# Block 2: expert weights go into the out-projection's buffers one by one, and the overflow loop moves from pair 25 to pair 28

## The chip, the cores and the metric

The kernel runs on one core of one Trainium2 chip. The metric is the time of one execution in device microseconds (us). The kernel before takes 3347.88 us (median of three runs, 3345.87 to 3349.38).

## What is computed

Two transformer blocks on 1024 tokens of width 1024, in float32. The change touches only the end of the second block: the product with `w_mla_o`, the merge of two branches, the product with `w_out`, the router, and 64 experts of hidden width 256, of which every token takes two. Cut to this part, the reference is:

```python
branch_b = o @ w_mla_o                                   # inside mla_attention
merged = sigmoid(g_a) * branch_a + sigmoid(g_b) * branch_b
h = h + merged @ w_out
u = rmsnorm(h, norm2_g)
g_logits, e_logits = u @ wg + bg, u @ we + be            # 8 groups, 8 experts in each
# best group; its best two experts; their weights
...
y = (silu(xb @ w1[e]) * (xb @ w3[e])) @ w2[e]            # for each expert e, the rows of its tokens
h = h + sum over a token's two experts of weight * y
```

An expert gets as many rows as the router gives it. The kernel provides 64 slots for each expert, and a loop for the rows beyond them.

## The kernel before

**Merge phase** (`phase3`, lines 1398 to 1427). The tokens are taken in two halves `b` of 512, and for each the 1024 output columns in eight steps `m` of 128. A step needs a slab of `w_mla_o`, 1024 x 128. Float32 products are made from operands that are split in a high and a low part (`wh`, `wl`), so a step has 8 x 3 matmuls. `slab2` brings a slab: the weights come by DMA, issued on SP, into a staging tile `ws` of 128 x 512 (256 KB), in two parts; ACT casts a part to `wh`, DVE subtracts to get `wl`, and then the staging tile is free for the next load. A tag with `bufs=2` in a pool is a ring of two buffers, and a load into a ring waits until the buffer's last user is done. The staging tile has `sbufs=2`. The results of the merge stand in four tiles: `mT0h`, `mT0l` (half 0) and `mT1h`, `mT1l` (half 1), each 16 KB in a partition.

Within the same loops the four slabs `ws[0]` to `ws[3]` of `w_out` (1024 x 256 each, in four parts of 256 KB) are brought, one at the steps 8b+m = 2, 5, 8 and 11. Before, they are made in pool `p3x` with a staging ring of their own there, while the slabs of `w_mla_o` stage in pool `p3y`. So 32 loads of 256 KB go through the one ring and 16 through the other.

**Out-projection** (`out2`, lines 1846 to 1885). Eight tiles `t` of 128 tokens: 96 matmuls with `mT` and the four `w_out` slabs, norm, router logits, and after tiles 3, 6 and 7 a part of the routing (`route_group`). Tiles 0 to 3 read `mT0`, tiles 4 to 7 `mT1`. SP brings a row tile `o_x` for every `t`.

**Experts** (`moe2`, lines 1888 to 1985). 32 pairs `p` of experts; a pair's weights are six DMAs of 1 MB (6.29 MB): gate and up for two experts (`n_w`) and down for two (`n_d`). There are six `wt` and six `dt` buffers, so three pairs are held; the weights of pair `p + 3` are loaded from POOL's queue when pair `p` has been used. `wt[0]` lies apart, all others are in a pool that takes the room of `p3x`, so it opens when `out2` is over: the waits are by tile, and a buffer waits for the old tiles that lay in the same place. SP issues the loads of pairs 0 to 2, POOL the rest. The rows of a pair are gathered by POOL (`n_x`, line 1009), turned on PE (`tp`), multiplied (`mm`), passed through ACT and DVE (`n_h`), turned and multiplied again, scaled (`n_y`) and added to the result by an indirect DMA from POOL (line 1015, "scatter" below).

**Overflow loop** (`overflow`, lines 1019 to 1127): a hardware loop over the count `v_ni` of blocks of rows beyond the slots; each engine loads `v_ni` (line 1059) and branches (line 1060). With these inputs its body is never run. It stands behind pair 25's scatter, ahead of the loads of pair 28.

The scheduler that puts instructions in order on each engine is not the program text's; the orders shown below are those of the built program.

Of the kernel before, what the change touches and what calls it, by code (L numbers as in the profile page):

```python
# [67 lines left out]
class Kern:  # L68
# [106 lines left out]
    def phase1a(self, keep, dram):  # L175
        """Modulation, norm, the projections of the mixer, and its gated linear attention among them."""
# [8 lines left out]
        # gate of the mixer, shift and scale of the second norm, gate of the experts  # L185
        self.rows = self.t(dram, [4, D], tag="rows")

        with tc.tile_pool(name="p1a", bufs=1) as pool, tc.tile_pool(name="p1a_ps", bufs=1, space=PSUM) as psum:
# [436 lines left out]
    def da_units(self, pool, psum, cp):  # L625
        tc, nc, a = self.tc, self.nc, self.a
        # lambda
# [14 lines left out]
        for qb in range(4):  # L642
            for h in range(4):
# [282 lines left out]
        # the logits from rows that are not normed yet: scale and shift in the router's weights and bias  # L926
# [23 lines left out]
    def turned(self, pool, psum, x, bufs=2):  # L950
        """x [P, D] -> [P, 8, 128], every 128 columns transposed"""
# [9 lines left out]
    def logits(self, pool, psum, x, rs, rw, rb, out, n, tbufs=2):  # L961
        """out = rs * (x @ rw) + rb for a tile of tokens"""
# [23 lines left out]
    def turn_cols(self, pool, psum, x, n, tag, split, rows=P):  # L986
        """x [rows, 128 n] -> xT [P, n, rows], xT[p, k] the column p * n + k of x: in two parts or as it is"""
# [25 lines left out]
    def scatter(self, dst, idx, src):  # L1013
        """rows of src added to those of dst, every index once or out of bounds"""
# [4 lines left out]
    def overflow(self, pool, psum, pre, rt, h2d, yd, wg, wu, wd, E, HID, cap, gain=None):  # L1019
        """The slots of an expert past its first cap, 128 at a time."""  # L1020
# [136 lines left out]
    def moe1(self, rt):  # L1157
        """Every expert's slots against its weights, float32 products in two parts."""
# [102 lines left out]
    # ---------------------------------------------------------------- block 2, mixer  # L1261
    def slab2(self, pool, segs, kk, n, bufs=2, tag="w", sbufs=2, parts=2):
        """Weights [P, kk, n] from column segments of DRAM views [P, kk, w], split in two parts."""
        nc = self.nc
        wh = self.t(pool, [P, 8, 256], F32R, tag=tag + "h", bufs=bufs) if kk * n == 2048 else None
        if wh is None:
# [8 lines left out]
        for h in range(0, kk, step):  # L1275
            st = self.t(pool, [P, step * n], tag=tag + f"s{step * n}", bufs=sbufs).rearrange("p (k n) -> p k n", k=step)
# [10 lines left out]
    def proj_T(self, psum, w, col, x, kk, fin):  # L1287
        """fin(token block, [P, 512] of W[:, col:col+128].T @ x), x [P, kk, S] and w split"""
# [8 lines left out]
    def phase3(self, dram, rt2_pool, close_m1, out):  # L1297
# [20 lines left out]
        with tc.tile_pool(name="p3u_ps", bufs=1, space=PSUM, reuse_waits="tile") as psum:  # L1318
# [4 lines left out]
            # recurrent branch  # L1323
# [3 lines left out]
            # gates of the two branches, and the recurrent branch's way out  # L1327
# [57 lines left out]
        # attention  # L1385
# [10 lines left out]
        # way out  # L1396
        with tc.tile_pool(name="p3x", bufs=1, reuse_waits="tile") as pool:
            mT = [[self.t(pool, [P, 8, 512], F32R, tag=f"mT{b}{n}") for n in "hl"] for b in range(2)]
            with tc.tile_pool(name="p3y", bufs=1, side="right", reuse_waits="tile") as p2, \
# [4 lines left out]
                for b in range(2):  # L1404
# [7 lines left out]
                    for m in range(8):  # L1412
# [16 lines left out]
            self.m2_w = [self.t(self.m2r_cm.__enter__(), [P, 2, 8, 256], tag="n_w0")]  # L1429
# [3 lines left out]
    def norms(self, pool, psum, uT, wi, z):  # L1433
        """The norms between the blocks, u in two parts, and its low-rank products z."""
# [14 lines left out]
        for t in range(NT):  # L1449
# [9 lines left out]
            # the second norm, of x rs: its sum of squares from that of x  # L1459
# [18 lines left out]
    def low_rank(self, pool, mq, psum, z, zT, kss, gz, t):  # L1478
        """The normed low-rank rows of a tile of tokens, turned and in two parts."""
# [18 lines left out]
    def lru(self, pool, wp, psum, uT, wi, gd):  # L1498
        nc, a = self.nc, self.a
        # c1 = -4 softplus(-lambda), softplus as max(x, 0) + log1p(exp(-|x|))  # L1500
# [27 lines left out]
        for f in range(8):  # L1528
# [19 lines left out]
            # a, and -expm1(2 log a) as tanh(-log a) (1 + a^2)  # L1548
# [10 lines left out]
            # gelu  # L1559
# [21 lines left out]
    def rope_tables(self, pool, mq):  # L1581
        """cos and sin of position * frequency, [P, NT, 32] each"""
# [304 lines left out]
    def moe2(self, rt):  # L1887
# [4 lines left out]
        with tc.tile_pool(name="m2w", bufs=1, reuse_waits="tile") as wp:  # L1892
# [40 lines left out]
            for p in range(2):  # L1933
                load(p)
# [110 lines left out]
```

## Time and profile before

| what | value |
|---|---|
| median of 3 runs | 3347.88 us (3345.87 to 3349.38) |
| span of the profiled execution | 3342.7 us; no time of its own is given beside the span, 5.2 us less than the median |
| PE busy | 2993.7 us, 90% of the span |
| DVE, ACT, POOL busy | 1768.0, 1370.7, 835.8 us |
| DMA | 705.55 MB, 211 GB/s over the span |
| the last quarter: merge 2540 to 2641, out-projection to 2763, routing to 2784, experts to 3342.7 | 802.7 us |

Times of the trace are microseconds from the span's start. An engine's busy time in a stretch says how full it is there; what it waits for is read from the rows that name the end of an idle time. PEclk is the granted TensorE clock as a share of 2.4 GHz. Where the DMA share is near 1, the 16 DMA engines have no room.

### The profile page before, as it was taken

The page shows a single profiled execution, that of the slowest core. Times are in us where ns is not written, and L with a number is a line of the kernel's source. Part 1 is how long each engine was busy: PE and PEld are TensorE (multiplying, and loading weights), DVE is VectorE, ACT ScalarE, POOL GpSimd, SP SyncE. Part 2 cuts the span into 40 slices and gives each one's busy share as a digit, 9 for nine tenths or more (in the row PEclk, how much of TensorE's full clock was granted, in tenths as well). Part 3 has the DMA queues.
Part 4 walks back from the last instruction along what each step waited for, and adds up shares of the span by engine and source line. Part 5 has one row for each costly group of instructions (what it writes and reads, how often), then busy time and mean ns, then how long its engine had stood idle before and what let it go on. Part 6 is the DMA issues. An engine that isn't in the chain of part 4 may idle for free.

```text
span 3342.7 us, 42770 instructions
## 1 busy us (share of the span) xinstructions
PE 2993.7 (90%) x15849; PEld 2195.4 (66%) x15849; DVE 1768.0 (53%) x3374; ACT 1370.7 (41%) x2247; POOL 835.8 (25%) x553
## 2 busy tenths in 40 slices
PE   7999999799978899889799999999998997877858
PEld 4988854677756666666487778788887893332323
DVE  4244332877668778778656731348886443111101
ACT  4345311555535566566556632236664211000001
POOL 1000011122223468767510000110001103333332
PEclk8999999799989899999899999999999998999979
DMA  6223376666569899899732253332235549999988
GB/s 212 91 80 95 92 226 198 178 166 173 137 225 317 285 330 343 285 359 343 234 118 76 76 208 96 120 96 73 69 83 179 178 173 346 407 386 363 390 334 301
DMA packets 282097, 705.55 MB, mean 211 GB/s; under 512 B 33760, under 2 KB 168060, under 8 KB 233116
## 3 DMA queue, kind: packets, MB, share of 16 engines
q1 hardware_dynamic: 231036, 462.13, 42.3%
q0 software_dynamic: 44160, 222.81, 18.4%
q10 hardware_dynamic: 6688, 17.83, 1.5%
q8 instruction: 127, 2.08, 0.3%
q14 instruction: 86, 0.70, 0.1%
HBM read 616.11 MB, written 99.11 MB: 214 GB/s over the span
## 4 chain that ended last, share of the span: by engine, by line
PE 41%; DMA 17%; DVE 9%; POOL 5%; ACT 4%; issue 4%; POOLq 0%; SPq 0%; DVEq 0%; ACTq 0%
PE mm L88 31%; DMA n_d<-exp_w 13%; POOL m_lo L1180 3%; PE s L88 2%; PE tp L88 2%; ACT m_hi L1179 2%; DVE m_lo L1180 1%; DMA x1d<-m_y,o_tok 1%; PE tp L999 1%; PE o L88 1%; PE gt L88 1%; PE tp L691 1%; PE lg L88 1%; DVE da_e L660 1%; POOL m_rs L101 1%
## 5 line engine op out<-in xcount | busy, mean ns | idle before, releaser
L1180 DVE TENSOR_TENSOR m_lo<-m_w,m_hi 128x2048 fp32r<-128x2048 f32 x160 | 430.3, 2703 | 78.9 <-ACT m_hi L1179 70.3
L1179 ACT CAST m_hi<-m_w 128x2048 fp32r<-128x2048 f32 x192 | 360.6, 1907 | 84.4 <-PE mm L88 74.0
L88 PE MATMUL mm<-n_w,n_xTf 128*64 128x512 f32 x1024 | 271.6, 645 | 79.5 <-DMA n_w<-exp_w 58.1
L88 PEld LDWEIGHTS mm<-n_w,n_xTf 128*64 128x64 f32 x1024 | 92.3, 149 | 252.7 <-issue 250.3
L88 PE MATMUL mm<-m_lo,m_xTh 128*96 128x512 f32 x512 | 205.5, 401 | 20.0 <-DVE m_lo L1180 19.9
L88 PE MATMUL mm<-m_hi,m_xTh 128*96 128x512 f32 x512 | 206.9, 404 | 0.0
L88 PE MATMUL mm<-uTh,wh 128*128 128x512 f32 x512 | 205.3, 401 | 0.0
L88 PE MATMUL mm<-m_hi,m_xTl 128*96 128x512 f32 x512 | 204.4, 399 | 0.0
L88 PE MATMUL mm<-uTh,wl 128*128 128x512 f32 x512 | 203.2, 397 | 0.0
L88 PE MATMUL mm<-uTl,wh 128*128 128x512 f32 x512 | 202.4, 395 | 0.0
L88 PE MATMUL mm<-wh,hTh 128*128 128x256 f32 (+1 forms) x608 | 177.6, 292 | 2.0 <-ACT wh L269 2.0
L1284 DVE TENSOR_TENSOR wl<-ws,wh 128x512 fp32r<-128x512 f32 x128 | 91.5, 729 | 164.9 <-ACT wh L1283 152.2
L88 PE MATMUL mm<-wl,hTh 128*128 128x256 f32 (+1 forms) x608 | 175.5, 289 | 0.5 <-DVE wl L270 0.5
L88 PE MATMUL mm<-wh,hTl 128*128 128x256 f32 (+1 forms) x608 | 175.1, 288 | 0.6 <-DVE hTl L324 0.6
L1967 DVE TENSOR_TENSOR n_h<-n_h,mm 128x256 f32<-128x256 f32 x32 | 13.5, 420 | 304.4 <-ACT n_h L1966 304.4
L1180 POOL TENSOR_TENSOR m_lo<-m_w,m_hi 128x2048 fp32r<-128x2048 f32 x32 | 159.6, 4989 | 52.0 <-ACT m_hi L1179 46.3
L1009 POOL DMA_INDIRECT m_x<-h2d,o_tok x32 | 129.2, 4038 | 156.3 <-PE tp L999 129.0
L1015 POOL DMA_INDIRECT x1d<-m_y,o_tok x32 | 149.8, 4681 | 48.8 <-DVE m_y L1226 42.7
L1966 ACT ACTIVATE n_h<-mm 128x256 f32<-128x256 f32 x32 | 12.3, 384 | 327.6 <-PE mm L88 327.6
L88 PE MATMUL mm<-m_lo,m_hTh 128*96 128x512 f32 x256 | 104.3, 420 | 34.8 <-POOL m_lo L1180 34.8
L88 PE MATMUL s<-da_k,da_q 128*128 128x512 f32 (+1 forms) x384 | 115.0, 409 | 17.7 <-DVE da_e L660 17.3
L1283 ACT CAST wh<-ws 128x512 fp32r<-128x512 f32 x128 | 77.7, 619 | 127.2 <-PE mm L88 51.5
(534 smaller groups left out, 7653.4 us busy)
## 6 DMA issues: line engine op xcount, KB each, us to landing
n_w<-exp_w POOLq DMA_DIRECT2D x112, 1024.0 KB, 16.9
m_w<-expert_w_gate SPq DMA_DIRECT2D x64, 1024.0 KB
m_w<-expert_w_up SPq DMA_DIRECT2D x64, 1024.0 KB
m_w<-expert_w_down SPq DMA_DIRECT2D x64, 1024.0 KB
n_d<-exp_w POOLq DMA_DIRECT2D x58, 1024.0 KB, 16.8
wada<-w_ada SPq DMA_DIRECT2D x48, 512.0 KB
da_k<-ks SPq DMA_DIRECT2D x64, 320.0 KB
n_w<-exp_w SPq DMA_DIRECT2D x12, 1024.0 KB
```

The source lines that it names most:

```text
L88: self.nc.tensor.matmul(out, l, r, start=start, stop=stop)
L101: nc.gpsimd.tensor_tensor(out, m, self.neghalf[:, 0:w], op=ALU.pow)
L660: nc.vector.tensor_scalar(e[:, c0:c0 + n], ps, 0.125, mx[:, m, b - 1:b] if b else None, op0=ALU.mult, op1=ALU.max, accum_out=mx[:, m, b:b ...
L691: nc.tensor.transpose(pt[:, i, :], e[:, ts(4 * g + i, P)], self.ident)
L999: nc.tensor.transpose(pt[:, k, :], xk[:, g + k, :], self.ident[0:rows, 0:rows])
L1009: return self.nc.gpsimd.indirect_dma_start(out=out, out_offset=None, in_=src, in_offset=bass.IndirectOffsetOnAxis(ap=idx, axis=0), bounds_ ...
L1015: return self.nc.gpsimd.indirect_dma_start(out=dst, out_offset=bass.IndirectOffsetOnAxis(ap=idx, axis=0), in_=src, in_offset=None, bounds_ ...
L1179: nc.scalar.copy(hi, w)
L1180: (nc.gpsimd if order[j][1] == 5 else nc.vector).tensor_tensor(lo, w, hi.bitcast(F32), op=ALU.subtract)
L1283: nc.scalar.copy(wh[:, r, :], st)
L1284: nc.vector.tensor_tensor(wl[:, r, :], st, wh[:, r, :].bitcast(F32), op=ALU.subtract)
L1967: nc.vector.tensor_tensor(h, h, ph[:, 1, :], op=ALU.mult)
```

## The change

- `slab2` gets two arguments. With `pair=True` the high and the low part of a slab stand in one tile `whl` of 16 KB in a partition; with `spool` the staging tile is made in another pool. The `w_out` slabs use both, with `spool=p2`. Tag and pool of their staging are then those of the `w_mla_o` slabs.
- Pool `p3x` stays open to the end. The six `wt` and six `dt` buffers are its tiles: `wt[1]` is `mT0h`, `dt[0:2]` the halves of `mT0l`, `wt[2]` and `wt[3]` are `mT1h` and `mT1l`, `wt[4]` and `wt[5]` the first two `whl`, `dt[2:6]` the halves of the other two.
- Pair 0's weights are loaded in `out2` after tile 3 (`m2_load(0)`); those of pair 1 and 2 in `moe2`, as before.
- The call of `overflow` moves from `p == 25`, ahead of `load(p + 3)`, to `p == 28`, behind `load(31)`.

```diff
-    def slab2(self, pool, segs, kk, n, bufs=2, tag="w", sbufs=2, parts=2):
+    def slab2(self, pool, segs, kk, n, bufs=2, tag="w", sbufs=2, parts=2, pair=False, spool=None):
...
+        if pair:
+            both = self.t(pool, [P, 2, kk, n], F32R, tag=tag + "hl", bufs=bufs)
+            wh, wl = both[:, 0], both[:, 1]
...
-            st = self.t(pool, [P, step * n], tag=tag + f"s{step * n}", bufs=sbufs).rearrange("p (k n) -> p k n", k=step)
+            st = self.t(spool or pool, [P, step * n], tag=tag + f"s{step * n}", bufs=sbufs).rearrange("p (k n) -> p k n", k=step)
...
-                            ws.append(self.slab2(pool, [wo[:, :, ts(len(ws), 256)]], 8, 256, bufs=4, parts=4))
+                            ws.append(self.slab2(pool, [wo[:, :, ts(len(ws), 256)]], 8, 256, bufs=4, parts=4, pair=True, spool=p2))
...
+                if t == 3:
+                    self.m2_w[1] = self.t(self.p3x, [P, 2, 8, 256], tag="mT0h")
+                    d = self.t(self.p3x, [P, 2, 2, D], tag="mT0l")
+                    self.m2_d[0:2] = [d[:, 0], d[:, 1]]
+                    self.m2_load(0)
...
-            for p in range(2):
-                load(p)
+            wt[2], wt[3] = (self.t(self.p3x, [P, 2, 8, HID], tag="mT1" + n) for n in "hl")
+            wt[4], wt[5], *d = (self.t(self.p3x, [P, 2, 8, HID], tag="whl", bufs=4) for _ in range(4))
+            dt[2:6] = [x[:, i].rearrange("p a b -> p (a b)").rearrange("p (k n) -> p k n", k=2) for x in d for i in range(2)]
+            load(1)
...
-                    if p == 25:
+                    if p + 3 < E // 2:
+                        load(p + 3, 2 if p + 4 == E // 2 else 1, nc.gpsimd)
+                    if p + 4 == E // 2:
                         self.overflow(pool, psum, "n_", rt, self.h4d, self.x3d, wg.rearrange("e d h -> (e d) h"),
...
-                    if p + 3 < E // 2:
-                        load(p + 3, 2 if p + 4 == E // 2 else 1, nc.gpsimd)
```

`m2_load` is the old inner function `load` without its special order for pair 1.

**SP, early in the merge phase.** `ws` are staging tiles, `x_tb` and `x_mg` the other inputs of the merge. Before:

```order
L1280 DMA ws_4561_22708<-w_out 128x2x256
L1280 DMA ws_4562_22712<-w_out 128x2x256
L1280 DMA ws_4563_22716<-w_out 128x2x256
L1419 DMA x_tb_22698<-tbd_14281 128x512
L1280 DMA ws_4567_22726<-w_mla_o 128x4x128
L1280 DMA ws_4564_22720<-w_out 128x2x256
L1420 DMA x_mg_22699<-mgd_14280 128x512
L1280 DMA ws_4568_22730<-w_mla_o 128x4x128
L1280 DMA ws_4588_22855<-w_out 128x2x256
```

Now:

```order
L1283 DMA ws_4560_22707<-w_out 128x2x256
L1426 DMA x_mg_22699<-mgd_14280 128x512
L1283 DMA ws_4561_22711<-w_out 128x2x256
L1283 DMA ws_4562_22715<-w_out 128x2x256
L1425 DMA x_tb_22758<-tbd_14281 128x512
L1283 DMA ws_4563_22719<-w_out 128x2x256
L1426 DMA x_mg_22759<-mgd_14280 128x512
L1283 DMA ws_4566_22725<-w_mla_o 128x4x128
```

All four parts of a `w_out` slab now stand ahead of the next part of `w_mla_o`; before, the two kinds alternated. The other three slabs read alike.

**SP, first weights of the experts.** Behind the loads of `out2`'s tiles, before:

```order
L1865 DMA o_x_24496<-hd_14278 128x1024
L1914 DMA n_d_4877_24831<-exp_w_2 128x2048
L1911 DMA n_w_4876_24830<-exp_w_2 128x2048 x2
L1914 DMA n_d_4878_24832<-exp_w_2 128x2048
L1914 DMA n_d_4881_24835<-exp_w_2 128x2048
L1914 DMA n_d_4884_24838<-exp_w_2 128x2048
L1911 DMA n_w_4879_24833<-exp_w_2 128x2048 x2
L1911 DMA n_w_4880_24834<-exp_w_2 128x2048 x2
L1911 DMA n_w_4882_24836<-exp_w_2 128x2048 x2
L1914 DMA n_d_4883_24837<-exp_w_2 128x2048
L1911 DMA n_w_4885_24839<-exp_w_2 128x2048 x2
L1914 DMA n_d_4886_24840<-exp_w_2 128x2048
```

Now, from the load for tile 4 on:

```order
L1872 DMA o_x_23965<-hd_14278 128x1024
L1912 DMA mT0h_23957<-exp_w_2 128x2048
L1915 DMA mT0l_23958<-exp_w_2 128x2048
L1912 DMA mT0h_23957<-exp_w_2 128x2048
L1915 DMA mT0l_23958<-exp_w_2 128x2048
L1872 DMA o_x_24216<-hd_14278 128x1024
...
L1915 DMA whl_24834<-exp_w_2 128x2048 x2
L1912 DMA mT1h_24830<-exp_w_2 128x2048 x2
L1912 DMA mT1l_24831<-exp_w_2 128x2048 x2
L1059 TENSOR_LOAD v_ni_26731
L1059 ISA x2
L1912 DMA whl_24832<-exp_w_2 128x2048 x2
```

Pair 0's last four loads moved ahead of the `o_x` of tile 5, and SP's load of the count `v_ni` now stands ahead of all six loads of pair 2 (the last row shown is the first of them); before, it stood behind them.

**POOL, around the loop.** `out<-n_y` is the scatter of a pair. Before, behind pair 25's gather:

```order
L1015 DMA out<-n_y_26512,o_tok_22527 1024x1024
L1911 DMA n_w_4879_24833<-exp_w_2 128x2048
L1059 TENSOR_LOAD v_ni_26543
...
L1060 UNCONDITIONAL_BRANCH
L1911 DMA n_w_4879_24833<-exp_w_2 128x2048
L1914 DMA n_d_4881_24835<-exp_w_2 128x2048
L1911 DMA n_w_4880_24834<-exp_w_2 128x2048 x2
L1914 DMA n_d_4884_24838<-exp_w_2 128x2048
```

Now, behind pair 28's scatter:

```order
L1912 DMA mT1h_24830<-exp_w_2 128x1024 x2
L1059 TENSOR_LOAD v_ni_26731
...
L1060 UNCONDITIONAL_BRANCH
L1912 DMA mT1l_24831<-exp_w_2 128x1024 x2
L1912 DMA mT1h_24830<-exp_w_2 128x1024 x2
L1912 DMA mT1l_24831<-exp_w_2 128x1024 x2
L1915 DMA whl_24834<-exp_w_2 128x2048 x2
```

One of six loads of pair 28 stood ahead of the loop; now two of the ten (half-size) loads of pair 31 do, and the other eight stand behind it.

## Rows read from the trace of the kernel before

**Rows 1.** Windows: length; PE, PEld, DVE, ACT, POOL busy (instructions); PEclk; DMA share; GB/s.
```profile
2540.00:2580.00 40.00, 40.00 (x177) 32.87 (x176) 24.67 (x34) 16.99 (x31) 8.59 (x6) 1.00 0.75 224
2580.00:2590.00 10.00, 3.78 (x17) 2.85 (x16) 7.29 (x12) 5.40 (x10) 3.02 (x2) 0.82 0.82 245
2600.00:2641.00 41.00, 39.73 (x169) 31.21 (x170) 21.80 (x30) 13.26 (x22) 9.31 (x7) 1.00 0.50 154
2763.00:2784.00 21.00, 4.21 (x29) 2.92 (x30) 13.42 (x79) 0.42 (x3) 5.57 (x9) 0.52 0.96 373
2820.00:3240.00 420.00, 325.78 (x1360) 126.68 (x1359) 51.77 (x94) 38.92 (x71) 139.25 (x186) 0.93 1.01 389
3240.00:3254.00 14.00, 0.00 (x0) 0.00 (x0) 0.00 (x0) 0.46 (x1) 0.00 (x0) 0.50 0.17 64
3280.00:3320.00 40.00, 37.24 (x174) 14.18 (x172) 5.99 (x11) 4.97 (x9) 14.69 (x20) 1.00 1.02 406
```

**Rows 2.** PE in order of time, the end of half 0 and start of half 1.
```profile
2583.07 0.39 PE L88 MATMUL mm<-oTh,wl 128*128 128x512 f32 x1
2589.68 1.22 PE L88 MATMUL mm<-oTh,wh 128*128 128x512 f32 x2 [6.22 <-ACT oTh L1410]
```

**Rows 3.** ACT in order of time, late merge phase: casts out of staging, idle time before.
```profile
2612.42 0.62 ACT L1283 CAST wh<-ws 128x512 fp32r<-128x512 f32 x1 [1.70 <-DMA ws<-w_mla_o]
2614.70 0.62 ACT L1283 CAST wh<-ws 128x512 fp32r<-128x512 f32 x1 [1.66 <-DMA ws<-w_mla_o]
...
2617.27 0.62 ACT L1283 CAST wh<-ws 128x512 fp32r<-128x512 f32 x1 [0.61 <-DMA ws<-w_mla_o]
2620.43 0.62 ACT L1283 CAST wh<-ws 128x512 fp32r<-128x512 f32 x1 [2.54 <-DMA ws<-w_mla_o]
2621.96 0.62 ACT L1283 CAST wh<-ws 128x512 fp32r<-128x512 f32 x1 [0.91 <-DMA ws<-w_mla_o]
```

**Rows 4.** Groups by line, 2540 to 2641: out<-in xcount, busy us, mean ns, idle before.
```profile
L1283 ACT CAST wh<-ws 128x512 fp32r<-128x512 f32 x44 | 26.7, 620 | 42.7 <-DMA ws<-w_mla_o 32.1 <-DMA ws<-w_out 4.7 <-PE mm L88 2.4
```

**Rows 5.** SP's issues in order of time, from out-projection to experts.
```profile
2737.13 15.93 SPq L1914 DMA_DIRECT2D n_d<-exp_w  x3
2757.28 11.14 SPq L1911 DMA_DIRECT2D n_w<-exp_w  x6
2777.91 0.33 SPq L1914 DMA_DIRECT2D n_d<-exp_w  x1
```

**Rows 6.** POOL and DVE in order of time, first pair.
```profile
2775.20 1.13 POOL L1009 DMA_INDIRECT n_x<-h4d,o_tok  x1 [10.26 <-DVE v_nb L1047]
...
2776.82 0.13 DVE L1056 CAST v_ni<-v_pe 1x1 int32<-1x1 f32 x1
...
2793.43 1.66 POOL L1911 DMA_DIRECT2D n_w<-exp_w  x3 [8.21 <-ACT n_h L1966]
```

**Rows 7.** The chain of what ended last: start, us, what; 23 pieces `n_d` to the loop.
```profile
2838.04 16.85 DMA n_d<-exp_w
...
3213.55 16.39 DMA n_d<-exp_w
...
3230.49 21.96 DMA n_d<-exp_w
3252.45 1.60 issue
```

**Rows 8.** POOL in order of time, around the loop.
```profile
3232.70 1.64 POOL L1015 DMA_INDIRECT out<-n_y,o_tok  x1 [0.30 <-issue]
3234.78 0.57 POOL L1911 DMA_DIRECT2D n_w<-exp_w  x1 [0.44 <-issue]
3254.39 0.55 POOL L1911 DMA_DIRECT2D n_w<-exp_w  x1 [19.04 <-ACT n_xTf L1005]
```

**Rows 9.** ACT in order of time, `n_y` of pairs 28 and 31.
```profile
3293.35 0.69 ACT L1978 ACTIVATE n_y<-mm,o_w 128x512 f32<-128x512 f32 x1 [3.51 <-PE mm L88]
...
3332.89 0.69 ACT L1978 ACTIVATE n_y<-mm,o_w 128x512 f32<-128x512 f32 x1 [4.37 <-PE mm L88]
```

More of the change, by code (lines that the diff above doesn't have):

```diff
@@ L1259, in moe1 @@
             down(E - 1, turn_h(E - 1, h))
-    def slab2(self, pool, segs, kk, n, bufs=2, tag="w", sbufs=2, parts=2):
+    def slab2(self, pool, segs, kk, n, bufs=2, tag="w", sbufs=2, parts=2, pair=False, spool=None):
         nc = self.nc
-        wh = self.t(pool, [P, 8, 256], F32R, tag=tag + "h", bufs=bufs) if kk * n == 2048 else None
-        if wh is None:
+        wh = self.t(pool, [P, 8, 256], F32R, tag=tag + "h", bufs=bufs) if kk * n == 2048 and not pair else None
+        if pair:
+            both = self.t(pool, [P, 2, kk, n], F32R, tag=tag + "hl", bufs=bufs)
+            wh, wl = both[:, 0], both[:, 1]
+        elif wh is None:
             wh = self.t(pool, [P, kk, n], F32R, tag=tag + f"h{kk}_{n}", bufs=bufs)
@@ L1395, in phase3 @@
         lg = self.t(rt2_pool, [P, NT, 72], tag="lg2")
-        with tc.tile_pool(name="p3x", bufs=1, reuse_waits="tile") as pool:
+        self.p3x_cm = tc.tile_pool(name="p3x", bufs=1, reuse_waits="tile")
+        pool = self.p3x = self.p3x_cm.__enter__()
+        if True:
             mT = [[self.t(pool, [P, 8, 512], F32R, tag=f"mT{b}{n}") for n in "hl"] for b in range(2)]
@@ L1426, in phase3 @@
                         if (8 * b + m) % 3 == 2 and len(ws) < 4:
-                            ws.append(self.slab2(pool, [wo[:, :, ts(len(ws), 256)]], 8, 256, bufs=4, parts=4))
+                            ws.append(self.slab2(pool, [wo[:, :, ts(len(ws), 256)]], 8, 256, bufs=4, parts=4, pair=True, spool=p2))
             self.m2r_cm = tc.tile_pool(name="m2r", bufs=1, side="right", reuse_waits="tile")
-            self.m2_w = [self.t(self.m2r_cm.__enter__(), [P, 2, 8, 256], tag="n_w0")]
+            self.m2_w, self.m2_d, self.m2_slabs = [None] * 6, [None] * 6, {}
+            self.m2_w[0] = self.t(self.m2r_cm.__enter__(), [P, 2, 8, 256], tag="n_w0")
             self.out2(dram, mT, ws, lg, rt2, out)
@@ L1884, in out2, with m2_load, gate_up, down @@
                         self.route_group(p2, psum, rt2, lg, 64, 8, self.cap2, *g)
+    def m2_load(self, p, halves=1, eng=None):
+        nc, a = self.nc, self.a
+        eng = eng or nc.sync
+        wg, wu, wd = a["exp_w1_2"][0], a["exp_w3_2"][0], a["exp_w2_2"][0]
+        es = p, p + 32
+        w = [self.m2_w[(2 * p + i) % 6] for i in range(2)]
+        d = [self.m2_d[(2 * p + i) % 6] for i in range(2)]
+        def gate_up(i, h):
+            k = slice(8 // halves * h, 8 // halves * (h + 1))
+            for j, m in enumerate((wg, wu)):
+                eng.dma_start(w[i][:, j, k, :], m[es[i]].rearrange("(p k) n -> p k n", k=8)[:, k, :])
+        def down(i):
+            eng.dma_start(d[i].rearrange("p k n -> p (k n)"), wd[es[i]].rearrange("(p k) n -> p (k n)", k=2))
+        if halves == 1:
+            for i in range(2):
+                gate_up(i, 0)
+                down(i)
+        else:
+            for h in range(halves):
+                gate_up(0, h)
+                gate_up(1, h)
+            down(0)
+            down(1)
+        self.m2_slabs[p] = [(w[i], d[i]) for i in range(2)]
     def moe2(self, rt):
@@ L1891, in moe2 @@
         wg, wu, wd = a["exp_w1_2"][0], a["exp_w3_2"][0], a["exp_w2_2"][0]
-        with tc.tile_pool(name="m2w", bufs=1, reuse_waits="tile") as wp:
-            slabs, xTs = {}, {}
-            wt, dt = self.m2_w + [None] * 5, [None] * 6
-            for n in ("w1", "d0", "d1", "w2", "w3", "d2", "w4", "d4", "d3", "w5", "d5"):
-                i = int(n[1])
-                if n[0] == "w":
-                    wt[i] = self.t(wp, [P, 2, 8, HID], tag="n_" + n)
-                else:
-                    dt[i] = self.t(wp, [P, 2, D], tag="n_" + n)
-            def load(p, halves=1, eng=nc.sync):
-                es = p, p + E // 2
-                w = [wt[(2 * p + i) % 6] for i in range(2)]
-                d = [dt[(2 * p + i) % 6] for i in range(2)]
-                def gate_up(i, h):
-                    k = slice(8 // halves * h, 8 // halves * (h + 1))
-                    for j, m in enumerate((wg, wu)):
-                        eng.dma_start(w[i][:, j, k, :], m[es[i]].rearrange("(p k) n -> p k n", k=8)[:, k, :])
-                def down(i):
-                    eng.dma_start(d[i].rearrange("p k n -> p (k n)"), wd[es[i]].rearrange("(p k) n -> p (k n)", k=2))
-                if p == 1:
-                    for f in (down, lambda i: gate_up(i, 0)):
-                        f(0)
-                        f(1)
-                elif halves == 1:
-                    for i in range(2):
-                        gate_up(i, 0)
-                        down(i)
-                else:
-                    for h in range(halves):
-                        gate_up(0, h)
-                        gate_up(1, h)
-                    down(0)
-                    down(1)
-                slabs[p] = [(w[i], d[i]) for i in range(2)]
-            for p in range(2):
-                load(p)
+        wt, dt, slabs, xTs, load = self.m2_w, self.m2_d, self.m2_slabs, {}, self.m2_load
+        if True:
+            wt[2], wt[3] = (self.t(self.p3x, [P, 2, 8, HID], tag="mT1" + n) for n in "hl")
+            wt[4], wt[5], *d = (self.t(self.p3x, [P, 2, 8, HID], tag="whl", bufs=4) for _ in range(4))
+            dt[2:6] = [x[:, i].rearrange("p a b -> p (a b)").rearrange("p (k n) -> p k n", k=2) for x in d for i in range(2)]
+            load(1)
             with tc.tile_pool(name="m2", bufs=1, reuse_waits="tile") as pool, \
@@ L1952, in moe2 @@
                 front(0)
-                for m in (dt[4], wt[5], dt[5]):
-                    m = m.rearrange("p a b c -> p (a b c)") if len(m.shape) == 4 else m.rearrange("p a b -> p (a b)")
-                    nc.gpsimd.tensor_copy(m[:, 0:1], rt["tok"][:, 0:1])
+                for m in (dt[4], wt[5][:, 0], dt[5]):
+                    nc.gpsimd.tensor_copy(m[:, 0, 0:1], rt["tok"][:, 0:1])
                 load(2)
```

1 line of the change is left out of this document (added).

## Prediction

> **What bounds the kernel now.** I read the windows of the last quarter first, then PE, ACT and SP in order of time, then the chain. The reader is to see three stretches with different limits.
>
> In the merge phase PE is full: 177 matmuls in 40 us from 2540, 39.7 busy of 41 from 2600 [rows 1]. So a step `m` of 24 matmuls takes 24 x 40/177 = 5.4 us, and any late slab of weights adds to the end. The one hole stands between the halves: PE ends half 0 at about 2583.5, and starts half 1 at 2589.68 after 6.22 us of waiting for the casts of `oTs` [rows 2]. But the staging is not far from the limit either: ACT's 44 casts of staged weights waited 42.7 us, 32.1 of it for `w_mla_o` loads [rows 4].
>
> Routing then leaves PE nearly idle, 4.2 of 21 us, while DMA is at 0.96 [rows 1]. From 2820 to 3240 the experts are bound by DMA: share 1.01 at 389 GB/s, PE 326 of 420 us busy [rows 1]. The chain there is nothing but loads of `n_d` by POOL, each released by the landing of the one a pair ago: 22 periods from 2838.04 to 3230.49, 17.84 us a pair; the last one is 16.94 [rows 7]. Around the overflow loop there is a hole: POOL's scatter of pair 25 is at 3232.70, its next load but one at 3254.39, with 19.04 us of idle time before it [rows 8]. The last load in flight is counted 21.96 us instead of some 16.4 [rows 7], and DMA has a share of 0.17 from 3240 to 3254 [rows 1]. After it the weights of pairs 26 and 27 are there, PE goes at its own pace, and the six last pairs follow quickly: pair 28's `n_y` is at 3293.35, pair 31's at 3332.89 [rows 9].
>
> **The change part by part.** *The staging ring (the largest term).* Before, the 16 loads of `w_out` had two buffers of their own. Now all loads of the phase go through one ring of two, and SP has the four parts of a `w_out` slab in front of the next `w_mla_o`. How fast a ring of two turns is to be seen late in the phase, where only `w_mla_o` loads are left: the casts of one buffer stand at 2612.42, 2617.27 and 2621.96, those of the other at 2614.70 and 2620.43 [rows 3]. A turn takes 4.85, 4.69 and 5.73 us, and the cast waited for the DMA each time, so this is the ring's own pace and not PE's. A turn brings two loads. A step needs one turn (two loads, 4.85 us, of its 5.4), a `w_out` slab two turns (9.7 us) in which no step's weights come.
>
> By hand: one slab in hand covers 5.4 us of the first `w_out` slab, which leaves 9.7 - 5.4 = 4.3 us of PE waiting. Then the stock is gone. The three steps up to the next `w_out` slab regain 3 x (5.4 - 4.85) = 1.65, so each of the other three slabs costs 9.7 - 1.65 = 8.05, together 24.2. Of the 28.5 us the hole between the halves takes up 6.2, since it was waiting anyway: **+22 us**. Bounds: if the ring never stands still, 42 loads (44 casts, two of them loaded before 2540) are 21 turns of 4.69, the last slab is ready at 2540 + 98.5 = 2638.5, and one step later the phase is over at 2644 instead of 2641: +3. If nothing hides, four slabs of two turns of 5.73 are +46. I take the value worked out by slabs, since the order in which SP issues keeps the ring from running ahead over several slabs. A slower clock after each wait (0.82 in the stretch with the hole [rows 1]) would be within the waits for the ring. All that follows is moved by this term; nothing behind it has room to absorb it, since `out2` needs the last `mT` tile and starts with PE at once.
>
> The Trainium skill, page "DMA: Bandwidth & Descriptors", section "Anatomy of one DMA", gives a DMA a fixed cost of about 2.0 us beside its bytes at 436 GB/s, fitted on POOL's path. By that a 256 KB load is an estimated 2.6 us, and with a cast, a subtraction and an issue a turn is about 4.3; this term would be +13 and the whole 3372. Its fixed part is why two buffers don't stream; the rows here have the longer turn, on SP's path, so the sum goes by the rows.
>
> *The loop, from pair 25 to 28.* What the wait consists of does not change: eight of the ten loads of pair 31 stand behind the loop on POOL, as five of six of pair 28 did, so POOL still goes through it with loads in flight, and no engine passes. I keep its length, from scatter to next load 3254.39 - 3232.70 = 21.7 us [rows 8]. What changes is which pairs run on which side. Pairs 26 to 28 now come ahead of it at DMA's pace, 16.9 to 17.84 us each; I take 17.2, nearer to the last periods. So scatter 28 is at 3232.70 + 51.6 = 3284.3 and the restart at 3306.0. From the restart to the third `n_y` behind it took 3293.35 - 3254.39 = 39.0 [rows 8, 9]; so pair 31's is at 3345.0 instead of 3332.89, +12. Pair 31's own weights, some 5.2 MB behind the loop, take 13 us at 406 GB/s [rows 1], and are needed only for the third pair: hidden. The last scatters meet an empty DMA: -1. So **+11 us** (+8 with 16.9 and a tail 3 us shorter, +14 with 17.84).
>
> *Pair 0 after tile 3.* 4.2 MB leave the stretch before routing. That alone buys nothing: PE's first expert product waits for the gather, issued at 2775.20 when the router is done [rows 6]. Less traffic may let that gather land up to 3 us sooner. Against it, pair 2's loads now stand behind SP's load of `v_ni`, which DVE makes at 2776.82 [rows 6]; before, SP issued most of them from 2757.28 on and the last at 2777.91 [rows 5]. So DMA has pair 1 alone until 2777 (6.29 MB, 17 us at 373 GB/s, over by about 2774), then a gap of some 4 us, then pair 2 until about 2794; pair 3's load comes from POOL at 2793.43 [rows 6]. The stream goes on from there as before: **0 us** (-3 for the gather, +4 for the gap).
>
> *The rest.* A high and a low part in one tile, or two `n_d` in one, change no count of instructions on the path: a pair's two `n_d` are read by the same products and come free together. 0.
>
> **Sum.** 22 + 11 + 0 = +33 on the profiled span, 3342.7 -> 3375.7. The span is 5.2 us under the median of the runs; that is kept, so 3347.9 + 33 = **3381 us**.
>
> **The rivals.** (1) *The shared ring turns fast enough, and the changed order helps: not slower.* With `w_out` loads no longer in flight beside `w_mla_o`, each load may land sooner (DMA was at 0.75 to 0.82 early in the phase [rows 1]). From a turn of 3.3 us on (five turns in three steps, 16.3 us) no step waits, and half 1's `oTs` can come early enough to close the hole of 6.2: -6. With the loop's +11 that is 3353, within the measurement. Against it: the turns of 4.7 to 5.7 were measured with DMA at 0.50 and no `w_out` load left. (2) *The wait at the loop shrinks,* because the last weights keep DMA busy through it. With no wait at all, POOL issues load 31 over one period up to 3284.3 + 17.2 = 3301.5, it lands 16.4 later at 3317.9 [rows 7], pair 31's products take some 12.5, and its `n_y` is at 3330: -3 instead of +12, so the end at 3347.9 + 22 - 4 = 3366. Against it: eight loads behind the loop. (3) *The ring recovers over several slabs,* and costs about 10, half way to its lower bound: 3369. For it: ACT was seldom late itself, its 44 casts are 26.7 us of 101 [rows 4]. (4) *Worse than the forecast:* turns of 5.7 and a clock that falls at each wait, 3395 and more.
>
> **How the numbers follow.** Chances: the forecast 0.66, rival 1 0.11, rival 2 0.10, rival 3 0.08, rival 4 0.05. The forecast's own range is 3373 to 3392 (ring 17 to 28, loop 8 to 14). The range 3357 to 3393 takes in rivals 2 and 3 and the dearer ring, and leaves out rival 1 and most of 4. A change under 0.2% (6.7 us) can't be told from none here. Faster needs rival 1 and a shorter wait at the loop besides, 0.06; the rest of rival 1 and a part of 2 at a small ring cost are within 0.2%, 0.07; slower 0.87.
>
> **What would show it.** The ring: in the merge phase four waits of PE of 4 to 9 us, each behind a run of four `w_out` casts, and `out2`'s first tile some 22 us later; wrong, if PE stays full from 2540 to 2641 but for the old hole. The loop: a hole of some 21 us without PE or DMA behind pair 28's scatter, with three pairs behind it at 12.5 to 13 us each; wrong, if weights land during it. Pair 0: its four loads between tiles 3 and 4, and a gap on DMA ahead of pair 2's loads; the first expert product no more than 3 us sooner against the router's end. The forecast fails most likely if the ring's turns are shorter than in the rows, or if PE had more than one slab in hand.

## Result and profile after

The changed kernel takes 3381.24 us (median of four runs, 3377.74 to 3391.39), the kernel before 3346.88 in the same series: a ratio of 1.011, 95% interval 1.0093 to 1.0127, so 31 to 43 us slower. Forecast: 3381, range 3357 to 3393. The profiled execution of the changed kernel is the longest of its four, with a span of 3389.6 us. 6.6 us of that lie ahead of everything that the change touches: the attention's last score matmul starts at 2533.5 there and at 2526.9 before. In the twelve kernels of this text, which differ only behind it, that start lies between 2526.9 and 2537.2, so from here on stages are compared and not times from the start. Their ends are read from rows like these; first the kernel before, by tile (`h_qr`, then `x_tb`), with count, shortest/median/longest ns, and first and last start:

```profile
L88 PE MATMUL s<-h_kr,h_qr x192: 277/387/480, 2250.4 to 2526.9; 128*128 128x512 f32 x96, 128*128 128x256 f32 x64, 128*128 128x384 f32 x32
L1421 DVE SCALAR_TENSOR_TENSOR x_tb<-x_tb,mm x16: 678/680/689, 2545.2 to 2641.1; 128x512 f32<-128x512 f32 x16
```

and the changed kernel, the same two:

```profile
L88 PE MATMUL s<-h_kr,h_qr x192: 277/387/481, 2257.3 to 2533.5; 128*128 128x512 f32 x96, 128*128 128x256 f32 x64, 128*128 128x384 f32 x32
L1427 DVE SCALAR_TENSOR_TENSOR x_tb<-x_tb,mm x16: 679/686/689, 2550.5 to 2676.6; 128x512 f32<-128x512 f32 x16
```

The last two times of each kernel bound the stage **merge**: 2641.1 - 2526.9 = 114.2 us before, 143.1 now. The later stage ends are POOL's. In the changed kernel (start, us, instruction, idle time before; 32 scatters in all, of pairs 25, 28 and 31 here):

```profile
2811.18 1.13 POOL L1009 DMA_INDIRECT n_x<-h4d,o_tok  x1 [10.27 <-DVE v_nb L1047]
...
2826.87 1.14 POOL L1912 DMA_DIRECT2D n_w<-exp_w  x2 [8.17 <-ACT n_h L1970]
...
3269.91 1.64 POOL L1015 DMA_INDIRECT out<-n_y,o_tok  x1 [0.30 <-issue]
...
3321.47 1.64 POOL L1015 DMA_INDIRECT out<-n_y,o_tok  x1 [1.92 <-issue]
3322.55 1.17 POOL L1912 DMA_DIRECT2D mT1h<-exp_w  x1
3324.56 0.56 POOL L1912 DMA_DIRECT2D mT1h<-exp_w  x1 [0.84 <-DMA n_w<-exp_w]
3341.82 1.05 POOL L1912 DMA_DIRECT2D mT1l<-exp_w  x2 [16.70 <-ACT n_xTf L1005]
...
3383.16 1.55 POOL L1015 DMA_INDIRECT out<-n_y,o_tok  x1 [10.87 <-DVE n_y L1983]
```

The rows of before that answer to them are those of [rows 6, 8]. So the stages are **router** (last `x_tb` to first gather), **first pair** (to pair 3's first load on POOL), **stream** (to the scatter of pair 25) and **end** (to the span's end). In us, for all kernels of this text (their names below):

| kernel | merge | router | first pair | stream | end | merge's end to span's end |
|---|---|---|---|---|---|---|
| before | 114.2 | 134.1 | 18.2 | 439.3 | 110.0 | 701.6 |
| changed | 143.1 | 134.6 | 15.7 | 443.0 | 119.7 | 713.0 |
| e1 own ring | 115.2 | 134.4 | 14.8 | 443.6 | 118.9 | 711.7 |
| e2 loop at 25 | 140.4 | 134.4 | 15.4 | 442.3 | 110.5 | 702.6 |
| e3 both | 114.7 | 134.2 | 15.1 | 443.3 | 109.4 | 702.0 |
| e4 ring of four | 118.3 | 134.3 | 15.4 | 443.2 | 119.6 | 712.5 |
| e5 filled waits | 136.6 | 136.7 | 14.4 | 443.1 | 118.9 | 713.2 |
| e6 no loop | 115.4 | 134.2 | 14.6 | 440.4 | 97.7 | 686.9 |
| e7 loop at 31 | 113.6 | 134.0 | 14.8 | 444.5 | 103.3 | 696.6 |
| e8 pair 2 early | 114.6 | 134.6 | 14.9 | 439.6 | 108.9 | 698.0 |
| e9 e7 and e8 | 114.9 | 134.3 | 15.2 | 439.4 | 103.2 | 692.1 |
| e10 loop at 22 | 112.8 | 134.6 | 15.8 | 455.9 | 98.2 | 704.5 |

Each row is one execution. Stages that no edit touches agree within 3 us over all twelve (merge with a ring of its own: 112.8 to 115.4); whole times scatter by 5 us and more. e2, whose merge phase is that of the changed kernel, has 140.4 there. The change costs 28.9 us in merge, gains 2.5 at the first pair, loses 3.7 in the stream and 9.7 at the end.

**The merge phase.** PE in order of time, those matmuls of the phase that waited over 0.6 us (the time and the releaser stand in brackets):

```profile
2565.85 0.80 PE L88 MATMUL mm<-oTh,wh 128*128 128x512 f32 x1 [4.55 <-ACT wh L1286]
...
2593.56 0.80 PE L88 MATMUL mm<-oTh,wh 128*128 128x512 f32 x1 [8.21 <-ACT wh L1286]
...
2610.80 0.80 PE L88 MATMUL mm<-oTh,wh 128*128 128x512 f32 x1 [3.36 <-ACT oTh L1416]
2612.68 0.79 PE L88 MATMUL mm<-oTl,wh 128*128 128x512 f32 x1 [1.09 <-DVE oTl L1417]
2616.89 0.80 PE L88 MATMUL mm<-oTh,wh 128*128 128x512 f32 x1 [1.70 <-ACT oTh L1416]
...
2651.96 0.79 PE L88 MATMUL mm<-oTh,wh 128*128 128x512 f32 x1 [10.10 <-ACT wh L1286]
```

Three long waits are for the cast of a `w_mla_o` slab, and the hole between the halves, one wait of 6.22 before [rows 2], is now three of 6.15 together. What stands ahead of such a wait is seen on SP, ahead of the last one (`x2` with 4.19 us: the second issue waited for its buffer):

```profile
2636.30 0.38 SPq L1283 DMA_DIRECT2D ws<-w_out  x1
...
2639.14 0.38 SPq L1283 DMA_DIRECT2D ws<-w_out  x1
...
2641.01 4.19 SPq L1283 DMA_DIRECT2D ws<-w_out  x2
...
2647.63 0.37 SPq L1283 DMA_DIRECT2D ws<-w_mla_o  x1
```

Four parts of `w_out`, one behind the other through two buffers, 11.3 us from the first to the next `w_mla_o`. The chain has the rest (start, us, what; L1425 is SP's load of `x_tb`):

```profile
2647.18 0.34 SPq L1425
...
2647.63 3.56 DMA ws<-w_mla_o
...
2651.29 0.63 ACT wh L1286
...
2651.96 24.58 PE mm L88 x96
```

The load takes 3.56 us to land, the cast 0.63, and then the four last steps have all they need. Not all of the 11.3 us is the ring's: DVE was done with the buffer of the third `w_out` part at 2646.03, but the `x_tb` load ahead on SP waited until 2647.18 for POOL, and the `w_mla_o` load stood behind it. Windows of the same phase show a second cost (columns as in [rows 1]):

```profile
2566.00:2570.00 4.00, 4.00 (x10) 3.09 (x11) 1.21 (x2) 0.62 (x1) 0.00 (x0) 0.50 0.64 198
2570.00:2580.00 10.00, 10.00 (x42) 8.11 (x41) 3.27 (x5) 2.39 (x4) 1.61 (x1) 0.90 0.36 106
2590.00:2600.00 10.00, 6.44 (x16) 5.02 (x17) 2.87 (x5) 2.60 (x5) 0.00 (x0) 0.53 0.56 165
2610.00:2620.00 10.00, 6.41 (x13) 3.92 (x14) 6.90 (x10) 4.88 (x9) 1.62 (x1) 0.50 0.68 219
2650.00:2660.00 10.00, 8.04 (x24) 6.39 (x25) 2.77 (x4) 2.47 (x4) 0.00 (x0) 0.63 0.51 150
```

Behind each wait the granted clock is near 0.5, TensorE's lower level, before it comes back (the two first rows), and the matmuls that stand alone take 0.80 us instead of 0.39. The whole phase, 131 us from 2546 on against 101 from 2540 before, has PE busy for 101.5 us and idle for 29.5; before it was 91.5 and 9.5. So of the 30 us some 20 are waits, and some 10 are the same matmuls run slower.

**At the loop**, the hole from scatter 28 (3321.47) to the next load (3341.82) is 20.35 us, against 21.7 before [rows 8]. Pair 31's `n_y` on ACT starts at 3380.8, 39.0 behind the restart. Two windows of the hole:

```profile
3321.50:3330.00 8.50, 0.00 (x0) 0.00 (x0) 0.00 (x0) 0.00 (x0) 2.77 (x3) 0.50 0.89 323
3330.00:3341.80 11.80, 0.69 (x2) 0.29 (x4) 0.43 (x1) 0.59 (x1) 0.00 (x0) 0.50 0.08 28
```

For the first 8.5 us DMA still works off what is in flight, at a share of 0.89; for the other 11.8 us it is at 0.08, all but idle.

### The profile page after: what moved, and what is told of

Same layout as the page of the kernel before. It is cut to its first block, busy times and chain, and to the rows that moved or that the text cites. A ratio compares the mean times of both kernels' runs of the same rounds, so it can differ in the third digit from the quotient of the medians.

```text
span 3389.6 us, 42767 instructions
## 1 busy us (share of the span) xinstructions
PE 3014.0 (89%) x15849; PEld 2203.2 (65%) x15849; DVE 1769.6 (52%) x3374; ACT 1371.2 (40%) x2247; POOL 837.0 (25%) x553
## 5 line engine op out<-in xcount | busy, mean ns | idle before, releaser
L1287 DVE TENSOR_TENSOR wl<-ws,wh 128x512 fp32r<-128x512 f32 x112 | 78.3, 711 | 159.1 <-ACT wh L1286 158.8
L1970 ACT ACTIVATE n_h<-mm 128x256 f32<-128x256 f32 x32 | 12.3, 384 | 339.0 <-PE mm L88 339.0
L88 PE MATMUL mm<-whl,n_xTf 128*64 128x512 f32 x320 | 87.2, 652 | 42.0 <-DMA whl<-exp_w 21.2
L88 PEld LDWEIGHTS mm<-m_lo,m_xTh 128*96 128x96 f32 x512 | 84.4, 165 | 56.6 <-DVE m_lo L1180 23.6
L88 PEld LDWEIGHTS mm<-wh,hTh 128*128 128x128 f32 x608 | 116.1, 191 | 7.4 <-issue 3.7
```

Source lines behind the costliest of these rows:

```text
L88: self.nc.tensor.matmul(out, l, r, start=start, stop=stop)
L1287: nc.vector.tensor_tensor(wl[:, r, :], st, wh[:, r, :].bitcast(F32), op=ALU.subtract)
L1970: nc.scalar.activation(h, ph[:, 0, :], AF.Silu)
```

## Experiments

**e1: a ring of its own for `w_out`.** The loop stays at 28.

```diff
-            st = self.t(spool or pool, [P, step * n], tag=tag + f"s{step * n}", bufs=sbufs).rearrange("p (k n) -> p k n", k=step)
+            st = self.t(spool or pool, [P, step * n], tag=("o" if spool else tag) + f"s{step * n}", bufs=sbufs).rearrange("p (k n) -> p k n", k=step)
```

> The changed kernel, but the staging of w_out has a ring of two buffers of its own in the same pool; the loop stays at pair 28. Theory (the shared ring makes PE wait in the merge phase, and the waits lower its clock): PE's waits for the casts of w_mla_o, 22.9 us in the changed kernel, go to under 1, the merge phase is as long as before (about 101 us), and the time falls by 26 to 30, to 3352 to 3357. Rival (the cost lies in the loop's place and in the early loads, the ring is innocent): no less than 3375.

Measured: 3357.8 us, ratio to before 1.0042 (1.0027 to 1.0057); 23 us less than the changed kernel by the ratios, a little short of the 26 to 30, and 0.8 us above the range. The trace has the stage at 115.2 instead of 143.1. PE's waits from 2540 to 2645 (total, times, longest):

```profile
PE mm L88 <- ACT oTh L1416: 7.7, 3, 6.0
PE mm L88 <- DVE wl L1287: 1.1, 2, 0.5
PE mm L88 <- DVE oTl L1417: 0.8, 1, 0.8
```

Not one wait for a cast of `w_mla_o` is left (two of 0.5 us for the low part `wl` are); the hole between the halves is. SP's order changed as well: parts of the two kinds take turns again. What the order does without the second ring is told by e4. The shared ring is the cause, and the rival falls.

**e2: the loop back at pair 25,** ring shared.

```diff
+                    if p == 25:
+                        self.overflow(pool, psum, "n_", rt, self.h4d, self.x3d, wg.rearrange("e d h -> (e d) h"),
...
                     if p + 3 < E // 2:
                         load(p + 3, 2 if p + 4 == E // 2 else 1, nc.gpsimd)
-                    if p + 4 == E // 2:
-                        self.overflow(pool, psum, "n_", rt, self.h4d, self.x3d, wg.rearrange("e d h -> (e d) h"),
...
```

> The changed kernel with the loop back at pair 25, ahead of the loads of pair 28; ring shared. Theory (the wait at the loop keeps its length, but three pairs more run ahead of it at DMA's pace): 8 to 12 us less, 3369 to 3373, and the hole at the loop about 21 us as in both kernels. Rival (the place makes no difference, since DMA's total bounds the experts): within 3 us of 3381.

Measured: 3377.7 us, ratio 1.0095 (1.0078 to 1.0113). That is above the forecast 3369 to 3373, and with intervals of about 6 us on either side the times alone can't part the theory from its rival. The stages can: end goes from 119.7 to 110.5, 9.2 less, and merge's end to span's end from 713.0 to 702.6. The hole is there at its old length; POOL, scatter 25 and the loads around it:

```profile
3264.40 1.64 POOL L1015 DMA_INDIRECT out<-n_y,o_tok  x1 [0.30 <-issue]
3266.46 0.58 POOL L1912 DMA_DIRECT2D mT1h<-exp_w  x1 [0.43 <-issue]
3286.07 0.55 POOL L1912 DMA_DIRECT2D mT1h<-exp_w  x1 [19.03 <-ACT n_xTf L1005]
```

3286.07 - 3264.40 = 21.7 us, as before.

**e3: both undone** (the edits of e1 and e2). What is left of the change is pair 0's early loads and the buffers one by one.

> Both undone: own ring, loop at pair 25. What is left of the change is pair 0's loads after tile 3 and the buffers one by one. Theory (that part gains 2 us at pair 0 and gives them back in a gap ahead of pair 2's loads): 3345 to 3350, no difference from the kernel before. Rival (the early loads gain once the ring is out of the way): 3338 to 3343. Rival (the load of the count ahead of pair 2's weights costs more): 3351 and more.

Measured: 3350.2 us, ratio 1.0017 (1.0004 to 1.0029); the median is 0.2 us above the first theory's range and the interval doesn't hold 1. The trace shows both halves of the theory: 3.1 us less at the first pair, 4.0 more in the stream, 702.0 against 701.6 from merge's end.

**e4: the shared ring with four buffers.** `sbufs=4` in both calls of `slab2` in the merge phase.

```diff
-                        wh, wl = self.slab2(p2, [wm[:, :, ts(m, P)]], 8, P)
+                        wh, wl = self.slab2(p2, [wm[:, :, ts(m, P)]], 8, P, sbufs=4)
...
-                            ws.append(self.slab2(pool, [wo[:, :, ts(len(ws), 256)]], 8, 256, bufs=4, parts=4, pair=True, spool=p2))
+                            ws.append(self.slab2(pool, [wo[:, :, ts(len(ws), 256)]], 8, 256, bufs=4, parts=4, pair=True, spool=p2, sbufs=4))
```

> The changed kernel with the ring still shared, but of four buffers instead of two. Theory (two loads a turn are too few): four loads a turn are 4 in 4.9 us where 3 steps and a slab need 10 in 16.3, so the waits of PE go to under 2 and the time is that of the own ring, 3352 to 3357. Rival (the order in which w_out stands ahead of w_mla_o costs, however deep the ring): half or more of the 29 us stays, 3366 and more.

Measured: 3363.73 us, ratio 1.0050 (1.0031 to 1.0070), 7 us over the theory's range and under the rival's. The stage is 118.3, 4.1 over before; PE's waits from 2540 to 2650:

```profile
PE mm L88 <- ACT oTh L1416: 7.6, 3, 5.5
PE mm L88 <- ACT wh L1286: 3.0, 2, 2.7
```

22.9 us of waits for casts have become 3.0, not under 2. So depth is what lacks, and not the order alone: here too SP issues the four parts of a `w_out` slab one behind the other, with no `w_mla_o` among them (2562.66 to 2569.77, 2580.39 to 2588.26). What is left against e1, 3.1 us, is near the scatter of the stages; the scheduler also placed the loads of the steps otherwise, so it can't be put down to one of the two.

**e5: PE kept busy during the waits.** Extra matmuls on old operands, into a PSUM bank that nothing reads.

```diff
+                        nf = {3: 16, 6: 32, 12: 40}.get(8 * b + m, 0)
+                        if nf:
+                            pf = self.t(psum, [P, 512], tag="fl")
+                            for k in range(nf):
+                                self.mm(pf, pw[:, k % 8, :], oh[:, k % 8, :], True, True)
+                        pw = wh
```

> The changed kernel (shared ring of two, loop at 28) with extra matmuls on PE, whose results go nowhere, in front of the three steps that waited longest: 16 ahead of step 3, 32 ahead of step 6, 40 ahead of step 12, so that PE is busy while it waits. Stage measured: from the last score matmul of the attention to the merge's last x_tb, 143.1 us in the changed kernel, 114.2 before. Theory (of the 28.9 us more, some 20 are waits, and some 9 the lower clock after them): the matmuls behind the filled waits keep 1.00 of the clock and the stage takes 136 to 140. Rival (the ring sets the time, so a slower PE only fills the waits): 142 to 144.5.

Measured: the stage takes 136.6 us, 6.5 less, though PE has 88 matmuls more to do: the theory's range. Windows of the phase:

```profile
2580.00:2590.00 10.00, 8.27 (x37) 6.53 (x35) 5.05 (x6) 3.25 (x6) 1.70 (x2) 1.00 0.65 201
2590.00:2600.00 10.00, 9.47 (x35) 7.67 (x36) 4.35 (x6) 2.99 (x6) 1.29 (x1) 0.83 0.42 119
2610.00:2620.00 10.00, 8.88 (x24) 5.97 (x24) 4.82 (x7) 4.38 (x8) 0.00 (x0) 0.62 0.83 264
2650.00:2660.00 10.00, 10.00 (x46) 8.26 (x44) 5.24 (x8) 3.01 (x5) 2.58 (x2) 1.00 0.52 160
```

The clock is still low mainly around the hole between the halves, which wasn't filled. The whole phase, from its first matmul to its last, in the changed kernel, in e2 (same merge phase) and here, and the extra matmuls `fl` (busy us, mean ns):

```profile
2544.77:2676.52 131.75, 102.20 (x388) 79.99 (x387) 59.70 (x82) 40.80 (x68) 21.60 (x15) 0.84 0.49 153
2543.14:2672.30 129.16, 99.35 (x388) 76.91 (x387) 59.56 (x82) 40.79 (x68) 21.00 (x15) 0.87 0.51 156
2542.47:2667.87 125.40, 116.15 (x476) 91.08 (x475) 60.61 (x82) 40.96 (x68) 20.31 (x15) 0.95 0.51 161
L88 PE MATMUL fl<-oTh,wh 128*128 128x512 f32 x88 | 20.4, 389 | 0.0
```

Idle time and filling together are 125.40 - 116.15 + 20.4 = 29.7 us, as long as the idle time of the other two (29.6 and 29.8); the phase's own matmuls take 116.15 - 20.4 = 95.8 us instead of 102.2 and 99.4. So the lower clock is no part of the waits; it comes on top. Against e2 the stage's gain is only 3.8 us. 2.1 us are lost again in the router stage (136.7), whose cause is open, and the whole time, 3380.43 with a ratio of 1.0100 (1.0084 to 1.0115), can't be told from the changed kernel's.

**e6: no loop.** e1 with the call of `overflow` left out.

> Own ring for w_out, and the overflow loop left out altogether (its body is run for no input here). Stage measured: from the merge's last x_tb to the end, 702.0 us with the own ring and the loop at 25, 711.7 with the loop at 28. Theory (behind the loop PE catches up on weights that have landed, so most of the hole of 21 us is got back where it stands at 25): 688 to 695, 7 to 14 less than with the loop at 25 and 17 to 24 less than at 28. Rival (the hole is lost in full wherever it stands): 680 to 682.

Measured: 686.9 us from merge's end, 1.1 under the range; 3330.61 us, ratio 0.9949 (0.9934 to 0.9964). Taken out, the loop gives back 15.1 us at pair 25 and 24.8 at pair 28. 3 us of each are from the stream (440.4 against 443.3 and 443.6): without a loop SP has no load of the count ahead of pair 2's weights, which fits e8 below. By the stage end alone it is 11.7 (109.4 - 97.7) and 21.2 (118.9 - 97.7). So at 25 about 10 of the hole's 21.7 us are got back behind it, not the most of it that the theory has, and at 28 none: the measurement lies between theory and rival, nearer to the theory.

**e7: the loop behind the last pair.** e1 with the call at `p == 31`.

> Own ring for w_out, and the loop behind the last pair's scatter, where no load is in flight and no pair waits. Same stage. Theory (the loop costs what is in flight when it is reached, and what then runs at DMA's pace): only the last scatter and the branch are left, 690 to 699, under both kernels by 2 to 11 us. Rival (the loop has a fixed cost of some 10 us in which DMA is idle, wherever it stands): 700 and more.

Measured: 696.6 us, in the theory's range, 5.0 under the kernel before and 5.4 under e3; the time is 3342.95, ratio 0.9994 (0.9985 to 1.0003), not to be told from before. By the ratios it is 8 us under e3. POOL's last scatters:

```profile
3308.63 1.65 POOL L1015 DMA_INDIRECT out<-n_y,o_tok  x1 [1.01 <-ACT n_xTf L1005]
3322.68 1.59 POOL L1015 DMA_INDIRECT out<-n_y,o_tok  x1 [12.41 <-DVE n_hTf L1005]
3328.87 1.55 POOL L1015 DMA_INDIRECT out<-n_y,o_tok  x1 [4.60 <-DMA out<-n_y,o_tok]
```

The last starts at 3328.87 and the span ends at 3341.2: 12.3 us for its landing and the branch, against 6.5 in the kernel before, where only the landing follows.

**e8: two loads of pair 2 ahead of the count.** e3, with pair 2's first gate and up issued behind `load(1)`.

```diff
             load(1)
+            for j, m in enumerate((wg, wu)):
+                nc.sync.dma_start(wt[4][:, j], m[2].rearrange("(p k) n -> p k n", k=8))
...
             for i in range(2):
-                gate_up(i, 0)
+                if p != 2 or i:
+                    gate_up(i, 0)
                 down(i)
```

> Own ring, loop at 25, and the first gate and up loads of pair 2 stand with pair 1's on SP, ahead of its load of the loop count; the other four of pair 2 stay behind it. Stage as above, 702.0 without the move, and its part from pair 3's first load to the scatter of pair 25, 443.3 us (439.3 before the change). Theory (the 3 us gained at pair 0 are lost in the gap on DMA ahead of pair 2's loads): the gap closes, the part takes 439 to 441 and the stage 698 to 700.5. Rival (the stream of the experts ends when it ends because of POOL's and PE's pace, not of DMA's start): 442 to 444 and 701 to 703.

Measured: stream 439.6, and 698.0 from merge's end: both in the theory's ranges. The time is 3342.32, ratio 0.9995 (0.9986 to 1.0004). The gap, first in e3:

```profile
2774.00:2778.00 4.00, 0.72 (x5) 0.26 (x4) 3.63 (x30) 0.00 (x0) 0.00 (x0) 0.50 0.26 110
2778.00:2782.00 4.00, 0.00 (x0) 0.00 (x0) 1.85 (x9) 0.00 (x0) 3.21 (x6) 0.50 0.36 88
```

then in e8:

```profile
2774.00:2778.00 4.00, 0.51 (x4) 0.26 (x4) 3.46 (x23) 0.00 (x0) 0.89 (x1) 0.50 0.61 256
2778.00:2782.00 4.00, 0.75 (x4) 0.75 (x5) 0.79 (x4) 0.00 (x0) 2.73 (x6) 0.50 0.60 168
```

The DMA share of these 8 us rises from 0.31 to 0.61, 2.4 us worth of DMA, and the stream is 3.7 shorter.

**e9: e7 and e8 together.**

> What the runs point to: the early loads of pair 0 kept, own ring for w_out, first gate and up loads of pair 2 with pair 1's, loop behind the last pair. Stage from the merge's last x_tb to the end: 701.6 us before, 696.6 with the loop at 31 alone, 698.0 with pair 2 early alone. Theory (the two gains lie in different places, the gap on DMA ahead of the stream and the hole behind it): 691.5 to 694, and a time 7 to 10 us under the kernel before. Rival (both are the same microseconds, since DMA sets the end): 695.5 to 697.

Measured: 692.1 us from merge's end, 9.5 under before, and a time of 3338.9, ratio 0.9969 (0.9957 to 0.9981): faster than both kernels: by the ratios 10 us under before and 47 under the changed one. The two gains add.

**e10: the loop at pair 22,** own ring; one run.

> Own ring, loop at pair 22 instead of 25. Stage as above: 702.0 us with the loop at 25, 711.7 at 28, 686.9 without it. Theory (a hole ahead of enough pairs costs the time in which DMA is idle, some 15 us; only where fewer than six pairs follow does PE's pace add to it): 700 to 704, no gain from going further ahead. Rival (every pair that the loop stands earlier saves the 3 us between DMA's pace and PE's): 690 to 694.

Measured: 704.5, half a us over the theory's range and far from the rival's. In this run there is nothing to gain further ahead.

## Why the prediction was right

**The ring.** *Forecast +22, measured +28.9 (26.2 in e2's trace; 23 by the times of e1 and the changed kernel).* The mechanism is shown by e1 and e4. Worked out by slab, the waits were 4.3, then 8.05 for each further slab; the trace has 4.55, 8.21, then none of its own at the third, whose slab falls into the hole between the halves, and 10.10. The idle time grew by 20.1 us against 22.3 by the sum. So turns of 4.85 us and one slab in hand described the ring well in the sum; the last slab took 11.3 us instead of 9.7, over 1 us of it behind `x_tb`, a load that shares SP's queue and that the sum left out. The step that was mis-sized is the sentence on the clock, "within the waits for the ring": by PE's busy time the same matmuls cost some 10 us more (7 in e2), and in e5 3.8 to 6.5 us of that went away with the waits filled. A likely way, not tried by itself: a step that is late on PE gives its weight buffer back late, and ACT's casts waited 10.7 us on PE, 2.4 before [rows 4].

By the fixed cost per DMA that the Trainium skill gives ("DMA: Bandwidth & Descriptors", "Anatomy of one DMA"), the term was an estimated +13. The page's figure is for POOL's path; a load from SP took 3.56 us in the chain above instead of the estimated 2.6, and the rows decided.

**The loop.** *Forecast +11, measured +9.7.* Term by term: period 17.2 (17.19: 51.56 for three pairs); hole 21.7 (20.35); restart to pair 31's `n_y` 39.0 (39.0); tail -1 (8.8 instead of 9.8 behind that `n_y`). Pair 31's eight late loads were hidden, as forecast. That the hole keeps its length and only its cover changes is shown by e2 and e6. One sign of the prediction, a hole "without PE or DMA", holds for 11.8 us of it alone: in the first 8.5 DMA still brings what is in flight.

**Pair 0 early.** *Forecast 0, measured +1.7:* +0.5, -2.5 and +3.7 in router, first pair and stream. The gain and the gap were both named, and e8 shows that the gap ahead of pair 2 takes the gain away.

**Sum.** The terms came to +33 and the stages to +40; the medians differ by 34.4. That the point forecast met the median to 0.3 us is partly luck: an error of 7 us in the ring lies inside the interval of 31 to 43. The forecast's own range also has a slip: ring 17 to 28 and loop 8 to 14 add up to 3373 to 3390, not 3392.

**The rivals.** 1 (the ring is fast enough) and 3 (it recovers) fall with the waits shown. 2 (the loop's hole shrinks) fell by the 20.35 us; but what it would have saved, worked out as 4 us against before for a loop without any wait, was too little: e6, without a loop, has 12.3 less in end than before. 4 is in part what came, a clock that falls at each wait, at a fraction of its price.

**Left open.** What the engines wait for in the 11.8 us of the hole in which DMA is all but idle, and what the loop's branch itself takes: e7 pays 5.6 us more in end than e6 with nothing but a scatter in flight.

## What to carry to other kernels

A ring of staging buffers has a throughput, depth over turn, and adding a second user to it is costed like adding work to an engine; here a second ring of two buffers of 256 KB (e1) took 28 us off the stage and 23 off the time. A loop in the middle of a stream of loads, though its body is never run, costs what the work behind it cannot catch up: here the hole was 20 to 22 us, and 12 of it stayed in the stage end with six pairs behind it, all of it with three; behind all work the loop cost 6. When a load is moved ahead, look for what is queued between it and the next one, since the gain can be lost there.

## What was not expected of the hardware

That waits of 4 to 10 us, on an engine that is otherwise full, cost a third to a half as much again in clock: 20 us more of waits came with 10 us more of busy time for the same 384 matmuls (7 in e2), with a granted clock of 0.50 to 0.63 in windows right behind a wait, and 0.83 to 1.00 behind waits that extra matmuls filled.
